# A hybrid encoder layer on one core: ScalarE's table load, the normalising of x, the memory norm and the start of the first scan head

## Chip, cores and metric

The kernel runs on one core of one Trainium2 chip. The metric is device time in microseconds (us) of one execution, and the median of the runs counts. Before the change it is 849.8 us (three runs, 849.77 to 851.0).

## What is computed

One encoder layer on x (512 tokens, width 1024, float32) and a memory of 256 tokens. For this change the first sub-layer matters:

```
h = rmsnorm(x, pre_mix_g)
aq, ak, av, hq, hf_fwd, hf_bwd, hi, hg = split_columns(h @ w_in)
att = axial_gqa_attention(apply_rope(aq), apply_rope(ak), av)
rec = hgrn2_group(hq, hf_fwd, hf_bwd, hi, hg, lb, out_g)     # 4 gated scan heads
x = x + rmsnorm(concat(att, rec) @ w_out, post_mix_g)
m = rmsnorm(mem, mem_norm_g)                                  # used by the second sub-layer
```

rmsnorm(x, g) is x · rsqrt(mean(x²) + eps) · g, with one factor r for each token. Cross-attention into m and a gated MLP with a small convolution follow; nothing in them changes.

## The kernel before, in words

**Arithmetic.** Each float32 operand of a product is split in two: a high part rounded to the matmul's type (ScalarE casts or scales, `hi`, `wh`) and the rest (VectorE subtracts, `lo`, `wl`). A product is then three matmuls, hi·hi, hi·lo, lo·hi (`mm3`, lines 135 to 137).

**Weights** come in 132 units of 128 x 1024. `issue()` (line 114) loads a unit into one of two `raw` buffers by a transfer of SyncE's queue, casts it on ScalarE (line 102) and subtracts on VectorE (line 103; units 28 to 41 on GpSimd). A `raw` buffer comes free with the subtraction of the unit two before. Units 0 to 3 feed the first projection (v), 4 to 6 the first scan head (q and its two gates, `hgrn_in(0)`), 7 to 10 the output gate (`put_sg`), then 11 to 13 scan head 1, and so on.

**Start.** x arrives transposed (`xt`, eight chunks kc of 128 x 512), together with the column `gcol` of pre_mix_g. WARM matmuls on constants (line 326) run until the first operands are there. `split_x(kc)` (lines 332 to 338) makes x·g in two parts: `nc.scalar.mul` by `gcol` on ScalarE, and one scalar_tensor_tensor (multiply, subtract) on VectorE. TensorE projects v from these raw parts (line 365), since r can be applied to a projection's result.

**r.** ScalarE squares the rows of x (line 378), GpSimd makes r (lines 153 and 154) and four diagonal tiles `diag_r` (line 382), TensorE spreads them over all partitions (line 385, ones times diagonal), and ScalarE copies the result to `r_bc` (line 387). v is scaled in `put_v` (line 430). The projections of head 0 also use raw x; `scaled` (line 435, VectorE) multiplies them by `r_bc`.

**The normalised x** (`hT`) for all later projections is made by `normalize(kc)` (lines 390 to 394), one for each chunk while head 0's projections are traced: VectorE makes t = xt·gcol·r_bc (line 392), ScalarE casts t (line 102), VectorE subtracts (line 103).

**Scan head h** (`hgrn_core`, lines 476 to 558): VectorE adds the two directions' keys (`ksum`, line 486), TensorE multiplies them with q (line 489), then seven levels follow. In each, VectorE updates queries and keys (line 525, twice), folds the gates (line 530) and takes the masked result over (line 531), ScalarE copies keys (line 496), and TensorE multiplies (line 499). Then come the two widest levels (lines 506 and 511 to 518), the output matmuls (537 to 539), a norm, the gate (line 549), and a turn (line 553).

**Memory norm** (`mem_norm`, lines 629 to 637): the gain and two blocks of 128 x 1024 come by transfers of GpSimd's queue (lines 148 and 634); ScalarE squares (line 188), GpSimd makes the factors (lines 153 and 154), VectorE scales (line 170).

**Order.** `weave` draws from two generators so that their announced progress stays level: the projections with the memory norm at their head (`mix_projections`), and the scan heads 0 to 2 (`cores`). From the traced program a scheduler sets the order of the instructions on each engine; at run time each engine takes its own in that order. `tc.issue_after(ins)` sets the instructions of a block behind `ins` on the engine of `ins`.

Of the kernel before, what the change touches and what calls it, by code (L numbers as in the profile page):

```python
# [14 lines left out]
ALU = mybir.AluOpType  # L15
# [3 lines left out]
P = 128  # L19
D = 1024  # L20
T = 512
# [10 lines left out]
TURN_STEP, MEM_TURN, UP_TURN = 0, (0, 4), (0, 2)  # L32
POOL_UNITS = frozenset(range(28, 42))
CORE_SHARE = 53.0
WARM = 4
LEVELS = (1, 2, 4, 8, 16, 32, 64)
ASK = 3
MIX_ORDER = (0, 2, 3, 1)
# [34 lines left out]
def layer(tc, io, out):  # L73
    nc = tc.nc
# [11 lines left out]
    def small():  # L86
        return sm.tile([P, 16], F32, name="small", tag="small")

    def bank(tag):
        return ps.tile([P, 512], F32, name="ps_" + tag, tag=tag)  # L90

    def big(shape, dt=F32):
        return b8.tile(shape, dt, name="big", tag="big")

    def tmp2(shape=(P, 512), dt=F32, tag="ta"):
        return t2.tile(list(shape), dt, name="tmp2", tag=tag, bufs=TMP_BUFS[tag])

    def tmp4(shape, dt=F32):
        return t4.tile(shape, dt, name="tmp4", tag="tmp4")

    def split(hi, lo, src, eng=None):
        nc.scalar.copy(hi, src)  # L102
        (eng or nc.vector).tensor_sub(lo, src, hi.bitcast(F32))  # L103
# [4 lines left out]
    def load_w():  # L108
        raw = rawp.tile([P, 1024], F32, name="raw", tag="raw")
        last_load[0] = nc.sync.dma_start(raw, io["w"][issued[0]]).ins  # L110
        issued[0] += 1
        return raw

    def issue():
        pool_unit = issued[0] in POOL_UNITS
        raw = load_w()
        wh = wp.tile([P, 1024], F32R, name="wh", tag="wh")
        wl = wp.tile([P, 1024], F32R, name="wl", tag="wl")
        split(wh, wl, raw, nc.gpsimd if pool_unit else None)
        pending.append((wh, wl))  # L120
# [7 lines left out]
    def unit(n):  # L128
        taken[0] += 1
        issue_ahead()  # L130
        wh, wl = pending.popleft()
        return wh.rearrange("p (k n) -> p k n", k=n), wl.rearrange("p (k n) -> p k n", k=n)

    def mm3(o, a, b, start, stop):
        nc.tensor.matmul(o, a[0], b[0], start=start, stop=False)  # L135
        nc.tensor.matmul(o, a[0], b[1], start=False, stop=False)  # L136
        nc.tensor.matmul(o, a[1], b[0], start=False, stop=stop)  # L137

    def blk(b):
        return slice(b * P, (b + 1) * P)  # L140
# [4 lines left out]
    def gains(*names, eng=None):  # L145
        g = big([P, 2, D])
        for i, name in enumerate(names):
            (eng or nc.gpsimd).dma_start(g[:, i, :], rows_bc(io[name], D))
        return [g[:, i, :] for i in range(len(names))]

    def rstd_of(ss, n, width):
        r = small()
        nc.gpsimd.tensor_scalar(r[:, :n], ss, 1.0 / width, EPS, op0=ALU.mult, op1=ALU.add)
        last_pow[0] = nc.gpsimd.tensor_tensor(out=r[:, :n], in0=r[:, :n], in1=nhalf[:, :n], op=ALU.pow).ins
        return r
# [13 lines left out]
    def scale_rows(xb, r, g, h, c):  # L169
        nc.vector.scalar_tensor_tensor(out=h[:, half(c)], in0=xb[:, half(c)], scalar=r, in1=g[:, half(c)],  # L170
                                       op0=ALU.mult, op1=ALU.mult)
# [14 lines left out]
    def row_rstd(xb, h):  # L186
        ss = small()
        nc.scalar.activation(h, xb, ACT.Square, accum_out=ss[:, 0:1])
        return rstd_of(ss[:, 0:1], 1, D)[:, 0:1]
# [32 lines left out]
    def new_act():  # L222
        return Act([big([P, 4, T], F32R) for _ in range(2)], [big([P, 4, T], F32R) for _ in range(2)])
# [23 lines left out]
    def proj_tm(act, tags, use, n=512):  # L247
        o = [bank(t) for t in tags]
        nk = 1024 // n
        for j in range(8 // nk):  # L250
            w = unit(nk)
            for b in range(len(tags)):
                for k in range(nk):
                    kc = nk * j + k
                    mm3(o[b][:, :n], act.get(kc, blk(b)), (w[0][:, k, :], w[1][:, k, :]), kc == 0, kc == 7)
                if kc == 7:
                    use(b, o[b])
                yield 3 * nk * MM * n / 512
# [41 lines left out]
    ident = const.tile([P, P], F32, name="ident")  # L300
    gcol = const.tile([P, KC], F32, name="gcol")
    ones = const.tile([P, P], F32, name="ones")
    nhalf = const.tile([P, 16], F32, name="nhalf")
    warm = tmp2()
    xt = [big([P, 4, T]) for _ in range(2)]
    nc.scalar.dma_start(gcol, io["gx"])
    nc.gpsimd.memset(ones, 1.0)
    nc.vector.memset(warm[:, :256], 0.0)
    nc.gpsimd.memset(nhalf, -0.5)

    def load_xt(kc, n):
        nc.sync.dma_start(xt[kc // 4][:, kc % 4:kc % 4 + n, :], io["xt"][:, kc:kc + n, :])
# [11 lines left out]
    warm_ps = bank("b")  # L324
    for _ in range(WARM):
        nc.tensor.matmul(warm_ps[:, :256], ones, warm[:, :256], start=True, stop=True)

    raw_act = new_act()

    after = []  # L330

    def split_x(kc):
        src = xt[kc // 4][:, kc % 4, :]
        hi, lo = raw_act.get(kc, slice(0, T))
        cast = nc.scalar.mul(hi, src, gcol[:, kc:kc + 1]).ins
        rest = nc.vector.scalar_tensor_tensor(out=lo, in0=src, scalar=gcol[:, kc:kc + 1], in1=hi.bitcast(F32),
                                              op0=ALU.mult, op1=ALU.subtract).ins
        return cast, rest
# [11 lines left out]
    v_ps = [bank(t) for t in "soso"]  # L350
    xr = room_x()
    ws = []
    for j in range(4):
# [7 lines left out]
        for k in range(2):  # L361
            kc = 2 * j + k
# [7 lines left out]
    ident_r = const.tile([P, P], F32R, name="ident_r")  # L370
    nc.vector.tensor_copy(ident_r, ident)
    taken[0] = 4
    for _ in range(2):
        issue()

    rx = const.tile([P, 2 * NB], F32, name="rx")
    for b in range(NB):
# [1 line left out]
    r = rstd_of(rx[:, :NB], NB, D)  # L379
    diag_r = tmp2((P, NB, P), tag="th")  # L380
    for b in range(NB):
        nc.gpsimd.tensor_scalar(diag_r[:, b, :], ident, r[:, b:b + 1], None, op0=ALU.mult)
    r_ps = bank("c")
    for b in range(NB):
        nc.tensor.matmul(r_ps[:, blk(b)], ones, diag_r[:, b, :], start=True, stop=True)
    r_bc = big([P, T])
    nc.scalar.copy(r_bc, r_ps)
    hT = new_act()

    def normalize(kc):  # L390
        t = tmp2()
        nc.vector.scalar_tensor_tensor(out=t, in0=xt[kc // 4][:, kc % 4, :], scalar=gcol[:, kc:kc + 1], in1=r_bc,
                                       op0=ALU.mult, op1=ALU.mult)
        split(*hT.get(kc, slice(0, T)), t)

    masks = const.tile([P, len(LEVELS), P], U8, name="masks")
    masks_f = tmp4([P, len(LEVELS), P])
# [23 lines left out]
    v = big([P, NB, T])  # L421
# [5 lines left out]
    sg_box, heads, qkv, rec_done = [], {}, {}, [0]  # L427

    def put_v(b, o):
        nc.scalar.mul(v[:, b, :], o, r[:, b:b + 1])  # L430

    def scaled(put):
        def use(o):
# [15 lines left out]
    def hgrn_in(h, between=(), raw=False):  # L449
        qk = big([P, 2, 2, T])  # L450
        tt = big([P, 2048])
        q = tmp2(tag="tq")

        def put_q(z):
            nc.scalar.activation(q, z, ACT.Sigmoid)
            nc.vector.tensor_mul(q, z, q)

        def put_f(d):
            def put(z):
                f = tt[:, d * T:(d + 1) * T]  # L460
                k = qk[:, 1, d, :]
                nc.scalar.activation(f, z, ACT.Sigmoid)
                nc.scalar.activation(k, z, ACT.Sigmoid, scale=-1.0)
                nc.vector.tensor_scalar(f, f, oml[:, d, h:h + 1], lb[:, d, h:h + 1], op0=ALU.mult, op1=ALU.add)
                nc.vector.tensor_scalar(k, k, oml[:, d, h:h + 1], None, op0=ALU.mult)
                nc.vector.tensor_mul(qk[:, 0, 1 - d, :], q, f)
            return put

        for put in (put_q, put_f(0), put_f(1)):
            yield from proj_fm(raw_act if raw else hT, T, "b", scaled(put) if raw else put)  # L470
            for job in between[:2]:
                job()
            between = between[2:]
        heads[h] = (q, qk, tt)
# [150 lines left out]
    tm_tags = ("s", "s", "o", "o")  # L625
# [3 lines left out]
    def mem_norm():  # L629
        g_mem, = gains("mem_norm_g")  # L630
        kv["rows"] = big([P, MB, D])
        for b in range(MB):
            m = kv["rows"][:, b, :]
            nc.gpsimd.dma_start(m, io["mem"][blk(b), :])
            r = row_rstd(m, tmp4([P, D]))
            for c in range(2):
                scale_rows(m, r, g_mem, m, c)
# [4 lines left out]
            turn_in(kv["rows"][:, b, :], kv["m"], b, "bb")  # L642

    def mix_projections():
        mem_norm()
        yield from proj_tm(hT, tm_tags, put_sg)
        yield from hgrn_in(1)
        yield from hgrn_in(2)
        mem_turn()
        yield from proj_tm(hT, tm_tags, put_kv, 256)  # L650
        late = []
        yield from proj_tm(hT, tm_tags, lambda b, z: late.append(lambda: put_qn(b, z)))
        yield from hgrn_in(3, late)

    def cores():
        for h in range(3):
            yield from hgrn_core(h)

    for b in range(NB):
        put_v(b, v_ps[b])  # L660
    for i, _ in enumerate(hgrn_in(0, raw=True)):
        if i < KC:
            normalize(i)
    weave((mix_projections(), 100.0), (cores(), CORE_SHARE))

    kT, vv, qT = qkv["kT"], qkv["vv"], qkv["qT"]
# [100 lines left out]
    hT = new_act()  # L767
# [75 lines left out]
    hT = new_act()  # L843
# [163 lines left out]
```

## Time and profile before

| | us |
|---|---|
| median of three runs | 849.8 |
| the profiled execution, its own time | 851.05 |
| its span, first to last instruction | 849.3 |
| TensorE busy | 828.8 (98% of the span) |
| VectorE busy | 526.6 (62%) |
| ScalarE busy | 401.1 (47%) |
| GpSimd busy | 95.9 (11%) |

The profile is of one execution; all its times count from the first instruction of its span. A row of the timeline has start, length, engine, line, operation, output and inputs, and in square brackets how long the engine was idle before it and what ended that. PE is TensorE, DVE VectorE, ACT ScalarE, POOL GpSimd, SP SyncE; a q behind the name (SPq) is the engine's queue. An engine's successive instructions overlap a little, so a start to the next start is somewhat less than a length.

### The profile page before, as it was taken

How to read it: one execution, taken by the hardware profiler on the slowest of the kernel's cores; microseconds unless marked ns; L12 is line 12 of the kernel's file. 1: busy time of each engine (PE TensorE's matmuls, PEld its weight loads, DVE VectorE, ACT ScalarE, POOL GpSimd, SP SyncE). 2: the span in 40 equal slices, each digit the busy share in tenths (PEclk: the TensorE clock that was granted, in tenths of full speed). 3: DMA queues.
4: the chain of work that ended last, by engine and by line, in shares of the span. 5: the costliest groups of instructions: out<-in, count | busy, mean ns of one | idle time of the engine just before them, and what ended most of it. 6: DMA issues, size and time to landing. Idle time of an engine off the chain costs nothing.

```text
span 849.3 us, 11048 instructions
## 1 busy us (share of the span) xinstructions
PE 828.8 (98%) x4304; PEld 702.9 (83%) x4304; DVE 526.6 (62%) x799; ACT 401.1 (47%) x710; POOL 95.9 (11%) x128
## 2 busy tenths in 40 slices
PE   8979999999999999999999999999999999999996
PEld 6868888887889888888888998888888888888885
DVE  5598497969997774854443865555555557722224
ACT  6563345445878884644543643333333335511121
POOL 0311100224243301300001300000000000000001
PEclk9999999999999999999999999999999999999999
DMA  9722202122222224252312242223233332322212
GB/s 323 232 76 75 74 25 87 51 76 75 75 75 91 78 81 175 75 174 75 100 50 75 76 135 98 95 94 100 100 100 99 100 100 79 101 96 97 100 49 100
DMA packets 24756, 83.52 MB, mean 98 GB/s; under 512 B 3264, under 2 KB 3904, under 8 KB 24704
## 3 DMA queue, kind: packets, MB, share of 16 engines
q1 hardware_dynamic: 22752, 77.44, 27.5%
q0 software_dynamic: 1232, 4.46, 1.7%
q10 hardware_dynamic: 720, 0.92, 0.3%
q8 instruction: 34, 0.56, 0.3%
q14 instruction: 18, 0.15, 0.1%
HBM read 80.71 MB, written 2.10 MB: 98 GB/s over the span
## 4 chain that ended last, share of the span: by engine, by line
PE 87%; DVE 6%; DMA 3%; ACT 2%; issue 1%; POOL 0%; POOLq 0%; DVEq 0%; ACTq 0%
PE ps_b L135 9%; PE ps_b L136 9%; PE ps_b L137 9%; PE ps_s L137 6%; PE ps_s L135 6%; PE ps_s L136 6%; PE ps_o L135 6%; PE ps_o L137 6%; PE ps_o L136 6%; PE ps_c L135 4%; PE ps_c L136 4%; PE ps_c L137 4%; PE ps_c L499 3%; DMA raw<-in_w_dram 2%; PE ps_o L717 2%; DVE big L525 1%
## 5 line engine op out<-in xcount | busy, mean ns | idle before, releaser
L103 DVE TENSOR_TENSOR wl<-raw,wh 128x1024 fp32r<-128x1024 f32 x114 | 139.4, 1223 | 219.7 <-ACT wh L102 219.6
L102 ACT CAST wh<-raw 128x1024 fp32r<-128x1024 f32 x128 | 134.6, 1052 | 243.5 <-PE ps_o L137 80.5
L135 PE MATMUL ps_b<-big,wh 128*128 128x512 f32 (+1 forms) x320 | 118.0, 369 | 0.0
L136 PE MATMUL ps_b<-big,wh 128*128 128x512 f32 (+1 forms) x320 | 116.6, 364 | 0.0
L137 PE MATMUL ps_b<-big,wl 128*128 128x512 f32 (+1 forms) x320 | 116.5, 364 | 0.0
L137 PEld LDWEIGHTS ps_b<-big,wl 128*128 128x128 f32 x320 | 60.3, 188 | 9.3
L135 PEld LDWEIGHTS ps_b<-big,wh 128*128 128x128 f32 x320 | 60.4, 189 | 9.1
L136 PEld LDWEIGHTS ps_b<-big,wh 128*128 128x128 f32 x320 | 60.4, 189 | 8.9
L163 POOL TENSOR_SCALAR small<-small 128x1 f32<-128x1 f32 x40 | 14.0, 350 | 440.6 <-ACT tmp L194 421.7
L135 PE MATMUL ps_s<-wh,big 128*128 128x512 f32 (+1 forms) x140 | 53.8, 384 | 0.0
L137 PE MATMUL ps_s<-wh,big 128*128 128x512 f32 (+1 forms) x140 | 53.4, 382 | 0.0
L136 PE MATMUL ps_s<-wl,big 128*128 128x512 f32 (+1 forms) x140 | 52.9, 378 | 0.0
L525 DVE TENSOR_TENSOR big<-big 128x512 f32<-128x512 f32 x64 | 49.8, 786 | 2.7 <-PE ps_c L499 1.6
L135 PE MATMUL ps_o<-wh,big 128*128 128x512 f32 (+1 forms) x124 | 47.5, 383 | 0.0
L137 PE MATMUL ps_o<-wh,big 128*128 128x512 f32 (+1 forms) x124 | 47.3, 381 | 0.0
L136 PE MATMUL ps_o<-wl,big 128*128 128x512 f32 (+1 forms) x124 | 47.1, 380 | 0.0
L103 DVE TENSOR_TENSOR big<-ps_o,big 128x512 fp32r<-128x512 f32 x52 | 35.8, 688 | 15.9 <-ACT big L102 15.5
L103 POOL TENSOR_TENSOR wl<-raw,wh 128x1024 fp32r<-128x1024 f32 x14 | 33.9, 2424 | 57.9 <-ACT wh L102 49.2
L102 ACT CAST big<-ps_o 128x512 fp32r<-128x512 f32 x52 | 30.4, 585 | 19.9 <-PE ps_o L814 7.5
L135 PE MATMUL ps_b<-wh,big 128*128 128x512 f32 x92 | 36.6, 398 | 0.0
L136 PE MATMUL ps_b<-wl,big 128*128 128x512 f32 x92 | 36.1, 392 | 0.0
L137 PE MATMUL ps_b<-wh,big 128*128 128x512 f32 x92 | 36.0, 391 | 0.0
(246 smaller groups left out, 1891.7 us busy)
## 6 DMA issues: line engine op xcount, KB each, us to landing
raw<-in_w_dram SPq DMA_DIRECT2D x131, 512.0 KB, 3.3
big<-in_x_dram SPq DMA_DIRECT2D x8, 512.0 KB, 7.3
big<-in_xt_dram SPq DMA_DIRECT2D x3, 512.0 KB, 8.0
big<-in_mem_dram POOLq DMA_DIRECT2D x2, 512.0 KB, 9.4
out_dram<-big SPq DMA_DIRECT2D x4, 256.0 KB, 2.1
out_dram<-big ACTq DMA_DIRECT2D x3, 256.0 KB, 2.1
big<-in_xt_dram SPq DMA_DIRECT2D x2, 256.0 KB, 3.4
raw<-in_w_dram SPq DMA_DIRECT2D x2, 256.0 KB, 4.0
```

The costliest lines, as they stand in the source:

```text
L102: nc.scalar.copy(hi, src)
L103: (eng or nc.vector).tensor_sub(lo, src, hi.bitcast(F32))
L135: nc.tensor.matmul(o, a[0], b[0], start=start, stop=False)
L136: nc.tensor.matmul(o, a[0], b[1], start=False, stop=False)
L137: nc.tensor.matmul(o, a[1], b[0], start=False, stop=stop)
L163: nc.gpsimd.tensor_scalar(ss[:, i + 4:i + 5], ss[:, i:i + 1], 1.0 / D, ss[:, i + 3:i + 4] if i else EPS, op0=ALU.mult, op1=ALU.add)
L499: nc.tensor.matmul(o[:, b, :], kc[:, blk(b)], pat(qk, b * P, [[2 * m, P // (2 * m)], [T + m, 2], [1, m]]), start=True, stop=True)
L525: nc.vector.tensor_tensor(out=c, in0=c, in1=pat(tt, toff + off, [[2, npair], [gap, 2], [0, m]]), op=ALU.mult)
L717: nc.tensor.matmul(o, vv[:, c, h // 4].rearrange("p a d -> p (a d)"), pt[:, j, c, :], start=c + j == 0, stop=c == 3 and j == 1)
```

## The change

Line numbers of the changed kernel are two higher than before from line 310 on, and nearly equal again from line 400 on. The diff, cut to its core:

```diff
-WARM = 4
+WARM, CORE_LEAD = 4, 3.0
...
     nc.gpsimd.memset(nhalf, -0.5)
+    table = small()
+    nc.scalar.copy(table, nhalf)
...
-    def split_x(kc):
+    def split_x(kc, act=raw_act):
         src = xt[kc // 4][:, kc % 4, :]
-        hi, lo = raw_act.get(kc, slice(0, T))
+        hi, lo = act.get(kc, slice(0, T))
...
     taken[0] = 4
-    for _ in range(2):
-        issue()
+    issue()
...
     for b in range(NB):
-        nc.gpsimd.tensor_scalar(diag_r[:, b, :], ident, r[:, b:b + 1], None, op0=ALU.mult)
+        nc.vector.tensor_scalar(diag_r[:, b, :], ident, r[:, b:b + 1], None, op0=ALU.mult)
...
-    nc.scalar.copy(r_bc, r_ps)
+    spread = nc.scalar.copy(r_bc, r_ps).ins
+    with tc.issue_after(spread):
+        issue()
     hT = new_act()
-
-    def normalize(kc):
-        t = tmp2()
-        nc.vector.scalar_tensor_tensor(out=t, in0=xt[kc // 4][:, kc % 4, :], scalar=gcol[:, kc:kc + 1], in1=r_bc,
-                                       op0=ALU.mult, op1=ALU.mult)
-        split(*hT.get(kc, slice(0, T)), t)
+    for i in range(4):
+        two = xt[i // 2][:, 2 * (i % 2):2 * (i % 2) + 2, :]
+        nc.gpsimd.tensor_tensor(out=two, in0=two, in1=r_bc[:, None, :].to_broadcast([P, 2, T]), op=ALU.mult)
...
     def mix_projections():
+        yield from proj_tm(hT, tm_tags, put_sg)
         mem_norm()
-        yield from proj_tm(hT, tm_tags, put_sg)
...
     def cores():
+        yield CORE_LEAD
         for h in range(3):
...
     for i, _ in enumerate(hgrn_in(0, raw=True)):
         if i < KC:
-            normalize(i)
+            split_x(i, hT)
```

So a copy of constants becomes ScalarE's first operation and brings the table load with it. Unit 5's cast stands behind the copy that makes `r_bc`. GpSimd multiplies xt by `r_bc` in place, in four instructions of 128 x 1024 (line 394), and `split_x` makes `hT` from that. The diagonal tiles are made by VectorE. The memory norm is traced behind the gate projection, and the scan heads announce 3.0 of progress before their first step.

On ScalarE, between the squares of x and the scaling of v (line 430), before the change:

```order
L378 ACTIVATE tmp_281,rx<-big 128x1024
L102 CAST wh<-raw 128x1024 x2
L415 ACTIVATE lbt<-lbt 128x16
L102 CAST wh<-raw 128x1024 x2
L387 COPY big<-ps_c 128x512
L430 ACTIVATE big<-ps_s,small 128x512
```

and with it, where L388 is the copy to `r_bc` and L337 the scaling in `split_x`:

```order
L379 ACTIVATE tmp_277,rx<-big 128x1024
L102 CAST wh<-raw 128x1024
L415 ACTIVATE lbt<-lbt 128x16
L388 COPY big<-ps_c 128x512
L102 CAST wh<-raw 128x1024
L430 ACTIVATE big<-ps_s,small 128x512
```

Three casts of weight units, 5 to 7, have moved from ahead of that copy to behind it.

On VectorE, the rows that lead to the first scan head (L486 is `ksum`), before:

```order
L103 TENSOR_TENSOR wl<-raw,wh 128x1024
L464 TENSOR_SCALAR big<-big,oml,lb 128x512
L465 TENSOR_SCALAR big<-big,oml 128x512
L466 TENSOR_TENSOR big<-tmp_332,big 128x512
L170 SCALAR_TENSOR_TENSOR big<-big,small 128x512 x4
L486 TENSOR_TENSOR tmp_520<-big 128x512
```

and where the memory norm's scaling (L170) stands now, far behind L486, which follows L466 at once; here L531 and L525 are steps of head 0's last levels, and L446 is the gate's product:

```order
L531 COPY_PREDICATED big<-masks,ps_c 128x4x128
L446 TENSOR_TENSOR big<-ps_o,tmp_674 128x512
L446 TENSOR_TENSOR big<-ps_o,tmp_695 128x512
L103 TENSOR_TENSOR wl<-raw,wh 128x1024
L170 SCALAR_TENSOR_TENSOR big<-big,small 128x512 x4
L525 TENSOR_TENSOR big<-big 128x2x2x128 x2
L103 TENSOR_TENSOR wl<-raw,wh 128x1024
```

The four L170 have moved from in front of the first head's first step to in front of its 128 wide level, for whose result TensorE's L511 waits. On VectorE from unit 5's subtraction to L486 there now stand six L103 of 128 x 1024, eight L338 (`split_x`), three L435, one L456, two each of L464, L465 and L466, and L486.

On GpSimd, from the masks (L409) on, with the change; before it the three transfers stood right behind L409 and no L394 existed:

```order
L409 CAST masks<-tmp_309 128x896
L394 TENSOR_TENSOR big<-big 128x1024 x4
L445 TENSOR_TENSOR tmp_643<-tmp_643,og 128x512
L148 DMA big<-in_mem_norm_g_dram 128x1024
L445 TENSOR_TENSOR tmp_653<-tmp_653,og 128x512
L634 DMA big<-in_mem_dram 128x1024
L445 TENSOR_TENSOR tmp_674<-tmp_674,og 128x512
L634 DMA big<-in_mem_dram 128x1024
L445 TENSOR_TENSOR tmp_695<-tmp_695,og 128x512
```

The memory's transfers have moved behind the products of the gate with its gain (L445), each of which waits for a sigmoid of the gate projection.

On TensorE, L489 (the first head's first product) stood behind 37 matmuls of the gate projection; it now stands behind 30 of its 96. L511 stood behind 84 of them; it now stands behind all 96 and 26 of the next projection.

More of the change, by code (lines that the diff above doesn't have):

```diff
@@ L429, in put_v @@
     def put_v(b, o):
-        nc.scalar.mul(v[:, b, :], o, r[:, b:b + 1])
+        return nc.scalar.mul(v[:, b, :], o, r[:, b:b + 1]).ins
     def scaled(put):
@@ L659, in layer @@
     for b in range(NB):
-        put_v(b, v_ps[b])
+        v_out = put_v(b, v_ps[b])
     for i, _ in enumerate(hgrn_in(0, raw=True)):
         if i < KC:
-            normalize(i)
+            split_x(i, hT)
     weave((mix_projections(), 100.0), (cores(), CORE_SHARE))
```

## The prediction

> **What bounds the kernel now.** TensorE is busy for 98% of the span, so what can be gained is where it waits or runs at a lower clock. I read TensorE's waits first, for the first 170 us, where every edit lies:
>
> ```profile
> PE ps_c L489 <- DVE tmp L486: 5.6, 1, 5.6
> ```
>
> One wait stands out: 5.6 us ahead of head 0's first product, for VectorE's `ksum`. The table by stretches shows what it costs besides (columns: length, then busy us of PE, PEld, DVE, ACT, POOL, then the granted clock):
>
> ```profile
> 50.00:56.00 6.00, 5.57 (x25) 4.29 (x23) 6.00 (x10) 3.67 (x7) 0.36 (x1) 1.00 0.28 90
> 56.00:62.00 6.00, 0.83 (x4) 0.83 (x5) 4.82 (x8) 2.26 (x4) 2.81 (x4) 0.90 0.28 87
> 62.00:70.00 8.00, 8.00 (x45) 7.09 (x45) 7.03 (x11) 3.19 (x5) 0.00 (x0) 0.86 0.19 66
> ```
>
> TensorE stands still in the second row, while the granted clock falls to 0.90 and then 0.86: 0.10 of 6 us and 0.14 of 8 us, another 1.7 us. VectorE was full before. Its timeline shows what stood in front of `ksum`:
>
> ```profile
> 57.24 1.41 DVE L170 SCALAR_TENSOR_TENSOR big<-big,small 128x512 f32<-128x512 f32 x2 [0.74 <-POOL small L154]
> 59.10 1.41 DVE L170 SCALAR_TENSOR_TENSOR big<-big,small 128x512 f32<-128x512 f32 x2 [0.44 <-POOL small L154]
> 60.43 0.68 DVE L486 TENSOR_TENSOR tmp<-big 128x512 f32<-128x512 f32 x1
> ```
>
> The memory norm, which nothing needs yet, holds VectorE for 4 us. The other place is the start, in the timeline of all engines:
>
> ```profile
> 0.72 0.40 ACTq L306 DMA_DIRECT2D gcol<-in_gx_dram  x1
> 1.26 3.75 PE L326 MATMUL ps_b<-tmp,ones 128*128 128x256 f32 x8 [1.26 <-DVE tmp L308]
> 3.81 1.28 ACT L335 ACT_TABLE_LOAD   x1 [3.81 <-DMA big<-in_xt_dram]
> 5.10 0.72 ACT L335 ACTIVATE big<-big,gcol 128x512 fp32r<-128x512 f32 x1
> 5.73 0.60 ACT L341 CAST wh<-raw 128x512 fp32r<-128x512 f32 x1
> 6.38 0.79 PE L365 MATMUL ps_s<-wh,big 128*128 128x512 f32 x1 [1.37 <-ACT wh L341]
> 9.11 0.63 PE L365 MATMUL ps_s<-wl,big 128*128 128x512 f32 x1
> 9.54 0.44 PE L365 MATMUL ps_o<-wl,big 128*128 128x512 f32 x1
> 9.81 0.40 PE L365 MATMUL ps_s<-wh,big 128*128 128x512 f32 x1
> ```
>
> The table load runs only once x has landed, 1.28 us on the path to the first matmul. And the first eight matmuls start 0.43 apart (9.11 to 9.54); the later ones take half of that.
>
> **The table load moved: -1.1 us.** It now runs before 3.8, while the transfers are under way. The first multiplication then waits for `gcol`, whose transfer took
>
> ```profile
> DMA to landing us min/median/max: 3.2/3.2/3.2
> ```
>
> from its issue at 0.72, so it starts at 3.92 instead of 5.10, and the first matmul at about 5.25 instead of 6.38. Bounds: 0 if the half unit of weights lands after 5.1, 1.28 at most. The second chunk's data are needed at a distance of 12 matmuls and have slack.
>
> **The clock at the start: -1.0 us.** TensorE's gap between warm-up and work shrinks from 1.37 to 0.25 us. In the rows the full pace came 3.4 us after the first real matmul; if that distance holds, nothing more is gained. If the warm-up now counts, up to eight steps fall from 0.43 to 0.23, 1.6 us. I take 1.0. The Trainium skill ("TensorE: Matmul & The Clock Gate", What's actually happening) states that the clock is released by one busy window of about 3.4 us, the windows running free of the kernel. By that rule the warm-up and the work would count together, and the sum would take the whole 1.6.
>
> **The diagonal tiles on VectorE, the copy ahead of unit 5's cast: 0.** These rows close the first projection:
>
> ```profile
> 29.54 0.39 PE L365 MATMUL ps_o<-wh,big 128*128 128x512 f32 x1
> 29.77 1.05 PE L385 MATMUL ps_c<-tmp,ones 128*128 128x128 f32 x8
> 30.58 0.48 PE L135 MATMUL ps_b<-big,wh 128*128 128x512 f32 x1
> 33.23 0.58 ACT L387 COPY big<-ps_c 128x512 f32<-128x512 f32 x1
> ```
>
> From 9.81 to 29.54 are 87 steps, 0.227 us each. L385 follows the last of them without idle time: its diagonal tiles are hidden behind the projection, on either engine. The copy, however, came 2.4 us after L385 had ended, behind casts that waited for weights; now it can follow at once. With the two gains at the start L385 begins near 27.7, and `r_bc` is there at 27.7 + 1.05 + 0.58 = 29.3. Unit 5's cast then ends near 30.3 rather than before 27; TensorE reaches that unit 24 matmuls (5.4 us) after 28.5, so the cast is covered by 3.6 us, less what follows.
>
> **x normalised by GpSimd: the wait for `ksum` comes back, +5.4 us, and half of the clock's loss, +0.9.** The work of VectorE on the way to `ksum`, by groups between 28 and 62 us (mean ns of one behind the comma):
>
> ```profile
> L103 DVE TENSOR_TENSOR wl<-raw,wh 128x1024 fp32r<-128x1024 f32 x5 | 6.1, 1221 | 5.2 <-ACT wh L102 5.2
> L392 DVE SCALAR_TENSOR_TENSOR tmp<-big,gcol 128x512 f32<-128x512 f32 x8 | 5.7, 743 | 0.0
> L435 DVE TENSOR_TENSOR tmp<-ps_b,big 128x512 f32<-128x512 f32 x3 | 2.0, 681 | 0.0
> L466 DVE TENSOR_TENSOR big<-tmp,big 128x512 f32<-128x512 f32 x2 | 1.4, 682 | 0.0
> L464 DVE TENSOR_SCALAR big<-big,oml,lb 128x512 f32<-128x512 f32 x2 | 1.1, 540 | 0.0
> L465 DVE TENSOR_SCALAR big<-big,oml 128x512 f32<-128x512 f32 x2 | 1.0, 478 | 0.0
> ```
>
> Eight L392 go (5.4 us at 0.08 less than a mean, the overlap of neighbours), and the L170 go. What stays, from unit 5's subtraction on: 6 x 1.14 (L103) + 8 x 0.67 (the new scalar_tensor_tensor, of L392's form) + 3 x 0.60 (L435) + 0.60 (L456) + 2 x (0.46 + 0.40 + 0.60) + 0.60 (L486) = 18.1 us. From 30.3 that would be done at 48.4. TensorE comes to L489 at 28.5 + (72 + 30) x 0.227 = 51.6, and would not wait.
>
> But the four multiplications on GpSimd meet this work. What happens then, other rows show:
>
> ```profile
> 238.24 2.70 POOL L103 TENSOR_TENSOR wl<-raw,wh 128x1024 fp32r<-128x1024 f32 x1 [3.44 <-DMA raw<-in_w_dram]
> 244.76 2.40 POOL L103 TENSOR_TENSOR wl<-raw,wh 128x1024 fp32r<-128x1024 f32 x1 [3.81 <-ACT wh L102]
> ...
> 238.00 0.68 DVE L525 TENSOR_TENSOR big<-big 128x512 f32<-128x512 f32 x1
> ...
> 239.62 0.69 DVE L103 TENSOR_TENSOR big<-ps_o,big 128x512 fp32r<-128x512 f32 x1
> 240.23 1.27 DVE L525 TENSOR_TENSOR big<-big 128x512 f32<-128x512 f32 x1
> ...
> 245.16 2.55 DVE L525 TENSOR_TENSOR big<-big 128x512 f32<-128x512 f32 x1
> ```
>
> An L525 with both inputs in SBUF takes 0.68 alone, but 2.55 when it starts 0.4 us into a GpSimd instruction of 2.40: it ends 0.55 after that one. The one at 240.23 ends likewise. The L103 at 239.62, which reads PSUM, is not held. And GpSimd, started during an L525, took 2.70. So the two run in turn, not together. L394 has the size of these 2.40 us instructions, and L445 takes half of that for half the size, with the same kind of broadcast operand:
>
> ```profile
> L445 POOL TENSOR_TENSOR tmp<-tmp,og x4: 1267/1276/1685, 81.8 to 87.3; 128x512 f32<-128x512 f32 x4
> ```
>
> Four of them are 9.6 us from 29.3 on. The first 1.0 passes before VectorE has unit 5's cast; the other 8.6 add to its 18.1: L486 ends at 57.0 instead of 48.4. The last `split_x`, ahead of L486, needs the last of them, so the order in which the two engines take turns does not change this. TensorE waits 57.0 - 51.6 = 5.4 us, at L489 or in part earlier (at unit 5's `wl`, or at unit 6 for the bank that the first L435 frees). Bounds: 3.6 if the three L435, which read PSUM, fall under GpSimd's turns, 0 if the engines overlap after all; I take 5.4, since of this work only the L435 read PSUM. The clock's 1.7 returns if the wait is in one piece, not if it is split; I take half. The Trainium skill ("SBUF - State Buffer", SBUF: two separate sides) calls this an exclusive lock, held for a whole instruction, and counts VectorE instructions with two SBUF inputs among those blocked; the 2.55 us above agrees.
>
> ScalarE multiplies (0.72) where it cast (about 0.63), 0.7 us in all, hidden behind its own idle time there.
>
> **The memory norm moved back: -5.6 and -1.7 for the old wait and its clock, +2.0 for a new one.** Its chain now begins with the gate's second sigmoid. Rows for it:
>
> ```profile
> 30.25 1.07 POOL L634 DMA_DIRECT2D big<-in_mem_dram  x2
> ```
>
> ```profile
> DMA to landing us min/median/max: 8.5/9.4/10.3
> ```
>
> ```profile
> raw<-in_w_dram SPq DMA_DIRECT2D x131, 512.0 KB, 3.3
> ```
>
> ```profile
> L188 ACT ACTIVATE tmp<-big x2: 1042/1044/1047, 54.4 to 55.4; 128x1024 f32<-128x1024 f32 x2
> ```
>
> ```profile
> L153 POOL TENSOR_SCALAR small<-small 128x1 f32<-128x1 f32 x2 | 1.7, 832 | 24.4 <-ACT tmp L188 24.3
> L154 POOL TENSOR_TENSOR small<-small,nhalf 128x1 f32<-128x1 f32 x2 | 1.5, 754 | 0.2
> ```
>
> Sigmoid 0.7 (as L335), L445 1.28, one issue 0.54, L445 1.28: the second block's transfer is issued 3.8 us after that sigmoid's matmuls. The same transfers took 9.4 us among the crowd at 30 us; a weight unit of their size takes 3.3. The queues are nearly empty there, so I take 4.0. Then the square 1.2, GpSimd 1.6, two L170 1.35, L525 0.7: 12.7 us in all. TensorE has 38 matmuls and three head products (0.81 each, as L385 to the next row) until L511: 11.0. So it waits 1.7, with GpSimd held up a little by VectorE 2.0; 1.0 to 7.1 by the transfer's bounds. While VectorE waits for these factors, L525, a unit's L103 and the next head's L456 queue behind L170; on ScalarE the copy of the head's wide result stands behind the square.
>
> **The sum.** -1.1 - 1.0 - 5.6 - 1.7 + 5.4 + 0.9 + 2.0 = -1.1 us, from 851.05 of the profiled execution. The median, 849.8, lies 1.25 below that one; I put the same -1.1 on it: **848.7 us**. A measurement here can tell about 0.2%, 1.7 us, from no change.
>
> **The rivals.**
> *The wait for `ksum` really goes* (0.26). GpSimd's work fits beside VectorE's, in its waits for casts and the L435. For it: VectorE had idle time there (5.2 us ahead of five L103). Against it: 240.23 and 245.16. Without 5.4 and 0.9: 842.4.
> *The memory's rows come late* (0.17), the slower side. If the transfers take the 9.4 us of before, L511 waits 7.1 instead of 2.0: 853.8. It turns slower by over 0.2% from a landing of 6.8 us on. For it: both were measured at 8.5 or more. Against it: the weights' 3.3.
> *The table load does not shorten the start* (0.07), since weights or the clock hold the first matmuls: 848.7 + 2.1 = 850.8.
>
> **How the numbers follow.** The forecast has 0.50, with a range of its own from 846.0 (L435 hidden, clock kept) to 851.0. Of it 0.19 lies below 848.1, 0.28 within 0.2% and 0.03 above 851.5. The first rival adds 0.26 to faster, the second 0.17 to slower, the third 0.04 to same and 0.03 to slower: faster 0.45, same 0.32, slower 0.23. The range, 842.0 to 853.0, takes in the first rival's time and most of the second's.
>
> **What would show it.** Right: the table load before 3.8; L365 from about 5.3; L394 of about 2.4 us, with L103 or L338 on VectorE beside them stretched to 2 us or more; TensorE waiting 4 to 6 us in all between 33 and 58 us for VectorE; one to three us ahead of L511. Wrong: L103 beside L394 at 1.22 and no wait at L489 (first rival); over 4 us ahead of L511 (second); the first L365 after 6.

## The result, and the profile after

The changed kernel takes 859.1 us (median of four runs, 857.0 to 859.5) against 849.8 before: a ratio of 1.0103, 95% interval 1.0083 to 1.0122, so about 9 us slower. Timed again on another chip it was 857.5 against 849.9: 1.0096 (1.0080 to 1.0112). The forecast was 848.7 and its range ended at 853.0.

The profiled execution after took 857.04 us with a span of 855.2. It is the fastest of its four, and the one shown of before (851.05, span 849.3) the slowest of its four, so the two traces lie only 6 us apart.

The start, from the timelines of ScalarE and TensorE (start, length, engine, line):

```profile
1.16 1.28 ACT L311 ACT_TABLE_LOAD   x1 [1.16 <-PEq L997]
...
3.83 0.72 ACT L337 ACTIVATE big<-big,gcol 128x512 fp32r<-128x512 f32 x1 [1.17 <-DMA gcol<-in_gx_dram]
...
5.11 0.79 PE L367 MATMUL ps_s<-wh,big 128*128 128x512 f32 x1
...
6.54 0.40 PE L367 MATMUL ps_o<-wh,big 128*128 128x512 f32 x1
6.77 0.40 PE L367 MATMUL ps_s<-wl,big 128*128 128x512 f32 x1
```

As forecast: the table load is out of the way, the first product comes at 5.11 instead of 6.38, and the full pace (0.23 from start to start) from 6.54 on instead of after 9.5. By 20 us the kernel is 2.1 us ahead of before.

TensorE's waits between 20 and 300 us (who waits, for whom; us in total, times, longest):

```profile
PE ps_b L135 <- DVE tmp L435: 4.8, 1, 4.8
PE ps_o L718 <- DVE big L103: 3.1, 3, 1.4
PE ps_c L499 <- DVE big L525: 2.7, 3, 1.3
PE ps_s L619 <- DVE tmp L103: 2.6, 2, 1.6
PE ps_c L511 <- DVE big L525: 1.8, 1, 1.8
PE ps_o L706 <- DVE big L103: 1.1, 2, 0.6
```

The 5.6 us at L489 are gone. In their place stands the wait that the forecast named, at unit 6 for the bank that L435 frees, and the one at L511. The other four rows are more than before had there (L717 1.9, L619 1.5, L499 0.7, none at L705). The first wait in the timeline of GpSimd and VectorE:

```profile
29.39 11.88 POOL L394 TENSOR_TENSOR big<-big 128x1024 f32<-128x1024 f32 x4 [1.29 <-ACT big L388]
...
30.29 2.60 DVE L103 TENSOR_TENSOR wl<-raw,wh 128x1024 fp32r<-128x1024 f32 x1 [2.14 <-ACT wh L102]
33.55 2.69 DVE L103 TENSOR_TENSOR wl<-raw,wh 128x1024 fp32r<-128x1024 f32 x1 [0.66 <-ACT wh L102]
36.16 6.33 DVE L338 SCALAR_TENSOR_TENSOR big<-big,gcol 128x512 fp32r<-128x512 f32 x3
...
43.54 0.68 DVE L435 TENSOR_TENSOR tmp<-ps_b,big 128x512 f32<-128x512 f32 x1
```

Four GpSimd instructions, of 2.4 us undisturbed, fill 11.88 us, and VectorE's subtractions, 1.22 alone, take 2.6 and more: one VectorE step to one of GpSimd, in turn.

So far all is near the plan, and yet 5 of the 6 us are still to come. The table by stretches, before (columns: length, busy us of PE, PEld, DVE, ACT, POOL, then the granted clock; the last line is the sum over 200 to 262 us):

```profile
210.00:220.00 10.00, 8.91 (x66) 8.44 (x66) 9.78 (x16) 7.88 (x15) 3.11 (x2) 1.00 0.18 54
230.00:240.00 10.00, 10.00 (x82) 9.61 (x81) 9.53 (x20) 8.83 (x19) 4.16 (x2) 1.00 0.28 100
...
sum 62.00, PE 57.29 PEld 52.49 DVE 57.56 ACT 46.76 POOL 23.60; mean PE 9.55 PEld 8.75 DVE 9.59 ACT 7.79 POOL 3.93
```

and after:

```profile
210.00:220.00 10.00, 8.37 (x53) 7.78 (x52) 9.86 (x10) 6.04 (x10) 5.20 (x2) 0.83 0.16 52
230.00:240.00 10.00, 7.30 (x58) 6.63 (x57) 10.00 (x18) 5.70 (x13) 3.59 (x2) 1.00 0.31 107
...
sum 62.00, PE 53.70 PEld 48.71 DVE 59.15 ACT 40.83 POOL 22.60; mean PE 8.95 PEld 8.12 DVE 9.86 ACT 6.80 POOL 3.77
```

TensorE does 57.29 - 53.70 = 3.6 us less in these 62 us, and ten of them run at a clock of 0.83, another 1.7. This is the start of attention beside scan head 3, over 100 us behind the work of the lines that the diff touches. VectorE is busy for 93% of it before and 95% after. The difference is in what it does while GpSimd makes the low part of a weight unit. After:

```profile
216.43 3.12 POOL L103 TENSOR_TENSOR wl<-raw,wh 128x1024 fp32r<-128x1024 f32 x1 [4.36 <-ACT wh L102]
228.30 2.39 POOL L103 TENSOR_TENSOR wl<-raw,wh 128x1024 fp32r<-128x1024 f32 x1 [8.75 <-ACT wh L102]
...
217.29 2.81 DVE L530 TENSOR_TENSOR big<-big 128x512 f32<-128x512 f32 x1
...
228.61 2.63 DVE L525 TENSOR_TENSOR big<-big 128x512 f32<-128x512 f32 x1 [0.54 <-PE ps_c L499]
```

and before:

```profile
226.36 2.41 POOL L103 TENSOR_TENSOR wl<-raw,wh 128x1024 fp32r<-128x1024 f32 x1 [4.72 <-ACT wh L102]
...
226.94 0.68 DVE L673 TENSOR_REDUCE small<-ps_s 128x1 f32<-128x512 f32 x1
227.53 0.68 DVE L103 TENSOR_TENSOR big<-ps_o,big 128x512 fp32r<-128x512 f32 x1
228.13 0.40 DVE L723 TENSOR_TENSOR tmp<-ps_o,tmp 64x256 f32<-64x256 f32 x1
```

Before, this subtraction falls beside VectorE steps that read PSUM (`ps_s`, `ps_o`), which run on at their 0.68. After, it falls on an L530 and an L525 whose inputs are both in SBUF, and each loses about 2 us. Summed over all of VectorE's rows between 200 and 262 us, the excess of the stretched ones (over 1.25 times the usual length of their form) is about 8 us before and 13.5 after. What GpSimd takes shows only as longer steps of VectorE: between 200 and 262 us of the changed kernel no wait that the profile lists for TensorE, VectorE or ScalarE ends with GpSimd or with a weight's transfer.

### The profile page after: what moved, and what is told of

It is laid out like the page before. It is cut to its first block, busy times and chain, and to the rows that moved or that the text cites. A ratio compares the mean times of both kernels' runs of the same rounds, so it can differ in the third digit from the quotient of the medians.

```text
span 855.2 us, 11032 instructions
## 1 busy us (share of the span) xinstructions
PE 829.8 (97%) x4304; PEld 704.0 (82%) x4304; DVE 536.2 (63%) x795; ACT 402.0 (47%) x711; POOL 106.0 (12%) x128
## 4 chain that ended last, share of the span: by engine, by line
PE 80%; DVE 7%; issue 6%; ACT 2%; DMA 2%; POOL 2%; SPq 0%; POOLq 0%; DVEq 0%
PE ps_b L137 8%; PE ps_b L135 8%; PE ps_b L136 8%; PE ps_s L136 6%; PE ps_s L137 6%; PE ps_s L135 6%; PE ps_o L135 5%; PE ps_o L137 5%; PE ps_o L136 5%; PE ps_c L136 4%; PE ps_c L135 4%; PE ps_c L137 4%; PE ps_c L499 2%; DVE big L525 2%; PE ps_o L718 2%
## 5 line engine op out<-in xcount | busy, mean ns | idle before, releaser
L103 DVE TENSOR_TENSOR wl<-raw,wh 128x1024 fp32r<-128x1024 f32 x114 | 142.2, 1247 | 212.1 <-ACT wh L102 212.0
L135 PE MATMUL ps_b<-big,wh 128*128 128x512 f32 (+1 forms) x320 | 118.8, 371 | 4.8 <-DVE tmp L435 4.8
L135 PEld LDWEIGHTS ps_b<-big,wh 128*128 128x128 f32 x320 | 60.9, 190 | 14.2 <-issue 5.2
L525 DVE TENSOR_TENSOR big<-big 128x512 f32<-128x512 f32 x64 | 53.8, 850 | 6.9 <-PE ps_c L499 4.7
L135 PE MATMUL ps_s<-wh,big 128*128 128x512 f32 (+1 forms) x140 | 54.1, 386 | 0.0
L135 PE MATMUL ps_o<-wh,big 128*128 128x512 f32 (+1 forms) x124 | 47.7, 385 | 0.0
L103 DVE TENSOR_TENSOR big<-ps_o,big 128x512 fp32r<-128x512 f32 x52 | 35.7, 686 | 16.0 <-ACT big L102 15.6
L103 POOL TENSOR_TENSOR wl<-raw,wh 128x1024 fp32r<-128x1024 f32 x14 | 34.8, 2486 | 62.1 <-ACT wh L102 51.8
L135 PE MATMUL ps_b<-wh,big 128*128 128x512 f32 x92 | 36.6, 398 | 0.0
```

The lines of the kernel that those rows point to most:

```text
L525: nc.vector.tensor_tensor(out=c, in0=c, in1=pat(tt, toff + off, [[2, npair], [gap, 2], [0, m]]), op=ALU.mult)
```

## Experiments

All ratios are to the kernel before, run on the same chip beside them, with the 95% interval; they go by all runs and can differ by 0.1% from the quotient of two medians. The theory after the comparison was A: the lead of the first core (`CORE_LEAD`) re-orders the whole stage from scan head 0 to scan head 3, and loses the time at 205 to 262 us. Its rivals were B, GpSimd's normalisation, and C, the memory norm.

**1. The table load alone**, on the kernel before.

```diff
+    table = small()
+    nc.scalar.copy(table, nhalf)
```

> Before, with the table load on a constant added and nothing else. Every theory expects the start's share alone: the load stands at about 1.2 us instead of behind the first tile, the first matmul of L365 comes about 1.2 us earlier, and the clock's early stretch costs less. 847.3 to 848.9 us (before: 849.8), unless an idle stretch later on eats it (then 849.8).

850.3 us, ratio 1.0003 (0.9990 to 1.0016): nothing. The trace (of an execution of 852.25 us, 2 us over the median) shows that the start does come earlier, by 1.8 us, and where the gain goes. Most of it goes before 31 us: TensorE comes to the diagonal tiles (L387 for L385) earlier than GpSimd has made them, and needs 2.2 us from its first L387 at 27.94 to L135, where it needed 0.8 before:

```profile
28.75 1.65 PE L387 MATMUL ps_c<-tmp,ones 128*128 128x128 f32 x6 [0.43 <-POOL tmp L384]
30.16 0.48 PE L135 MATMUL ps_b<-big,wh 128*128 128x512 f32 x1
```

The rest goes by 62 us, where the wait at `ksum` (here L491 for L488) is 6.3 us instead of 5.6. (The other piece, 0.4 us, stands ahead of scan head 3; before had 1.1 there.)

```profile
PE ps_c L491 <- DVE tmp L488: 6.7, 2, 6.3
```

ScalarE's timeline shows what that wait hangs on:

```profile
32.87 1.05 ACT L102 CAST wh<-raw 128x1024 fp32r<-128x1024 f32 x1 [5.72 <-DMA raw<-in_w_dram]
34.13 1.06 ACT L102 CAST wh<-raw 128x1024 fp32r<-128x1024 f32 x1 [0.21 <-DMA raw<-in_w_dram]
35.09 0.58 ACT L389 COPY big<-ps_c 128x512 f32<-128x512 f32 x1
```

`r_bc` (L389 here) stands behind two weight casts that wait for their transfers, and comes at 35.09 us, later than before (33.23) although TensorE has started earlier.

**2. The normalisation back on VectorE, the lead kept.**

```diff
-    for i in range(4):
-        two = xt[i // 2][:, 2 * (i % 2):2 * (i % 2) + 2, :]
-        nc.gpsimd.tensor_tensor(out=two, in0=two, in1=r_bc[:, None, :].to_broadcast([P, 2, T]), op=ALU.mult)
+    def normalize(kc):
+        t = tmp2()
+        nc.vector.scalar_tensor_tensor(out=t, in0=xt[kc // 4][:, kc % 4, :], scalar=gcol[:, kc:kc + 1], in1=r_bc,
+                                       op0=ALU.mult, op1=ALU.mult)
+        split(*hT.get(kc, slice(0, T)), t)
...
-            split_x(i, hT)
+            normalize(i)
```

> After, with the normalisation of x put back on VectorE as in before (no L394 on GpSimd, two VectorE steps and one ScalarE copy per chunk); table load, diagonal on VectorE, the moved memory norm and the lead of the first core stay. Theory A (the lead's new order of the mix stage loses the time at 205 to 262 us): the GpSimd stretch is gone and with it the wait of 4.8 us at L135 for L435, but the old wait at L489 comes back, so 855 to 859 us, little changed. Theory B (GpSimd's hold on VectorE sets everything later back): most of the loss goes, 848 to 852 us.

852.3 us, ratio 1.0024 (1.0011 to 1.0036): between the theories. GpSimd costs a good 6 us here, and the kernel is still slower than before. The old wait at L489, which A expected back, is only 0.7 us in this trace.

**3. Lead and memory norm back.**

```diff
-WARM, CORE_LEAD = 4, 3.0
+WARM, CORE_LEAD = 4, 0.0
...
-        yield from proj_tm(hT, tm_tags, put_sg)
         mem_norm()
+        yield from proj_tm(hT, tm_tags, put_sg)
```

> After, with the lead at 0 and the memory norm back at the head of the projections, so that only the table, the diagonal, the issue order and GpSimd's normalisation are changed. Theory A (the lead): about 850 to 853 us, the loss at 205 to 262 us is gone, since the order of the three tensor-side engines is that of before from the 260th row of TensorE on. Theory B (GpSimd's normalisation): 856 to 860 us, as after.

851.3 us, ratio 1.0013 (1.0002 to 1.0024): as A expected.

**4. The lead alone back** (the first pair of lines of that diff).

> After, with the lead of the first core at 0 and nothing else undone: the memory norm stays behind the gate's projection, the normalisation stays on GpSimd. Theory A (the lead): 850 to 854 us, within 1 us of the kernel that has the memory norm back as well. Theory B (GpSimd's normalisation) and theory C (the memory norm's late rows): 856 to 860 us; under C the kernel with the memory norm back is faster than this one by over 2 us.

849.9 us, ratio 0.9998 (0.9986 to 1.0010): A again, though 0.1 us under its range and 1.5 us from run 3 where it allowed 1; the lead costs 1.0096 - 0.9998 (the first from run 5), about 1% or 8.3 us. C falls: the moved memory norm is worth a little (0.15%, 1.3 us) rather than costing anything. The wait of 4.8 us at L135 stands in this kernel's trace as in the changed one's; the wait at L511 does not. By line and shape, the rows of TensorE, VectorE and ScalarE follow the order of before from 93 us on in this trace, and in the changed kernel's only from 239 to 249 us on.

That left a square with one corner open: without lead and without GpSimd's normalisation. A theory I, that each covers the other's wait, expected about 849; simple addition expected 843.

**5. The changed kernel again**, for the same chip.

> The changed kernel as it is, beside the others on the same chip: 857 to 860 us by every theory.

857.5 us, ratio 1.0096 (1.0080 to 1.0112).

**6. Lead and normalisation both back** (the edits of 2 and 4).

> After with the lead at 0 and the normalisation on VectorE both undone; table, diagonal on VectorE, issue order and the moved memory norm stay. It completes the square of lead and normalisation. Theory I (each wait covers the other: without the lead, GpSimd's normalisation puts the wait of 4.8 us at L135 in the place of the one of 5.6 us at L489, so that it costs next to nothing there, and costs 6.8 us only where the lead has taken the L489 wait away): 848 to 850 us, about the 849.9 of the kernel with the lead alone undone, and a wait of 5 to 6.5 us at L489. Theory S (the costs simply add, 9.2 us for the lead and 6.8 for GpSimd): 843 us.

843.3 us, ratio 0.9923 (0.9910 to 0.9935). Theory I falls: the costs add. The square, in per cent against before:

| | VectorE normalises | GpSimd normalises |
|---|---|---|
| no lead | -0.77 | -0.02 |
| lead of 3.0 | +0.24 | +0.96 |

The lead costs 1.0 in either column (8.3 to 8.6 us), GpSimd 0.7 to 0.75 in either row (6.1 to 6.4 us). And what is left of the change beats the kernel before by 6.6 us. The wait for head 0's `ksum` is gone altogether: the only one that its trace lists stands at 206.9 us, ahead of scan head 3, and before had the like there (1.1 us at 214.9):

```profile
PE ps_c L491 <- DVE tmp L488: 1.1, 1, 1.1
```

**7. and 8. GpSimd's weight subtractions replaced**, with the lead and without it. Both leave out the low part of units 28 to 41: it is set to zero.

```diff
-        split(wh, wl, raw, nc.gpsimd if pool_unit else None)
+        if pool_unit:
+            nc.scalar.copy(wh, raw)
+            nc.gpsimd.memset(wl.bitcast(F32), 0.0)
+        else:
+            split(wh, wl, raw)
```

> After, leaving out one piece of the computation: for the 14 weight units whose low part GpSimd subtracts (units 28 to 41), it writes zeros by a memset instead, in the same place of the same order, so that GpSimd reads nothing there. Theory D (the lead loses its time at 205 to 260 us because GpSimd's 2.4 us subtractions of L103 fall on more VectorE steps there, which this run's VectorE rows show stretched by 13.5 us in all, against 8.1 in before and 6.8 with the lead undone): it gains clearly more than the same cut in the kernel without the lead, so that the two lie 2 to 5 us apart instead of 9.2; about 848 to 852 us. Theory E (the lead's order itself runs dry there, whatever GpSimd does): gains as much as the other and stays 8 to 10 us above it.

> The same cut (zeros by a memset for GpSimd's 14 subtractions) in the kernel with the lead at 0. Both theories expect a gain from VectorE's stretches that go (6.8 us of stretches between 200 and 262 us, of which TensorE feels a part): 844 to 848 us. Theory D: this lies 2 to 5 us under the same cut with the lead; theory E: 8 to 10 us under it.

With the lead 846.4 us, ratio 0.9959 (0.9946 to 0.9971); without it 843.4, 0.9928 (0.9915 to 0.9942). Both gain more than either theory expected (848 and 844 us at the least). The two lie 3.0 us apart instead of 8.3: theory D. By line and shape, the order of 7 on TensorE, VectorE and ScalarE is the changed kernel's, row for row, so the order alone doesn't run dry there. The memsets still run on GpSimd, 0.96 us each:

```profile
L121 POOL MEMSET wl<- 128x1024 f32 x10 | 9.6, 956 | 48.1 <-PE ps_b L141 48.1
```

They read nothing, and VectorE's L525 beside them (mean ns behind the comma, between 200 and 262 us) is no longer stretched. After, then the same line, L529, in the lead's kernel with the memsets:

```profile
L525 DVE TENSOR_TENSOR big<-big 128x512 f32<-128x512 f32 x13 | 15.1, 1170 | 0.7 <-PE ps_c L499 0.5
```

```profile
L529 DVE TENSOR_TENSOR big<-big 128x512 f32<-128x512 f32 x16 | 11.6, 740 | 1.2 <-PE ps_c L503 0.6 <-PE ps_c L510 0.3 <-ACT tmp L500 0.2
```

The Trainium skill ("SBUF — State Buffer", Who interferes with whom) states just this: a VectorE instruction with two SBUF inputs contends with a GpSimd instruction that reads SBUF, not with one that only writes it. The 1,170 and 740 ns agree. The stage as a whole, TensorE's busy time between 200 and 262 us (first number behind the length), in the kernel of 4 (no lead, as 8 but with GpSimd's subtractions), then in 7, then in 8:

```profile
200.00:262.00 62.00, 56.94 (x427) 52.44 (x426) 57.34 (x102) 46.06 (x91) 21.26 (x9) 1.00 0.23 77
```

```profile
200.00:262.00 62.00, 61.71 (x460) 57.54 (x460) 56.99 (x115) 50.69 (x99) 11.71 (x12) 1.00 0.26 86
```

```profile
200.00:262.00 62.00, 62.00 (x465) 58.00 (x465) 55.12 (x113) 52.43 (x104) 9.23 (x10) 1.00 0.27 86
```

Without GpSimd's reads the stage is full with the lead (61.71) as without it (62.00); with them it holds 53.70 with the lead and 56.94 without. The 3 us that the lead still costs lie earlier: counted by matmuls, 7 is 2.8 us behind 8 at the 1,000th (192.9 and 190.1 us) and 3.4 at the 1,400th, while the changed kernel is 2.7 behind run 4's at the 1,000th and 8.0 at the 1,400th. L511 (1.7 us in 7's trace, none in 8's) is the largest part seen. The memset is also shorter than the subtraction that it replaces; as nothing waited for GpSimd in that stretch, this by itself doesn't explain the gain.

**9. and 10. What made the 6.6 us of gain?** From the kernel of 6, first the memory norm back (9):

```diff
-        yield from proj_tm(hT, tm_tags, put_sg)
         mem_norm()
+        yield from proj_tm(hT, tm_tags, put_sg)
```

and, apart from that, the issue order back (10):

```diff
-    issue()
+    for _ in range(2):
+        issue()
...
-    with tc.issue_after(spread):
-        issue()
```

> The kernel of 843.3 us (after with the lead at 0 and the normalisation on VectorE) with the memory norm back at the head of the projections, so that table, diagonal on VectorE and issue order are what is left of the change. Theory O (the issue order takes the wait of 5.6 us at L489: the spread copy of the row factors starts at 29.07 us instead of 35.09 behind two weight casts that wait for their DMA, and VectorE's normalisation with it): 843.5 to 846 us, the wait at L489 under 3.5 us. Theory M (the memory norm does, whose two scalings of 1.4 us stood ahead of L486 on VectorE): 848 to 850 us, the wait at L489 5 us or more.

> The kernel of 843.3 us with the issue order alone undone: both weight units are issued ahead of the squares again, and their casts stand ahead of the spread copy on ScalarE; table, diagonal on VectorE and the moved memory norm stay. Theory O (issue order): the spread copy starts at 33 to 35 us again, the wait at L489 is back with 3 to 5 us, 847 to 850 us. Theory M (memory norm): no wait over 2 us there, 843 to 845 us.

9 took 848.4 us, ratio 0.9980 (0.9971 to 0.9989); 10 took 846.7, 0.9969 (0.9956 to 0.9981). Both matter: 0.57% (4.8 us) for the memory norm and 0.46% (3.9 us; 3.1 by the medians) for the issue order. Together they are more than 6.6, so the parts don't simply add; the table and the diagonal were not taken out alone. By the time of 9 theory M had it, but not by its mechanism: no wait stands at `ksum`, but one of 3.1 us at L135. That the two scalings hold `ksum` up is not tested here, since in 9 the scheduler set them behind it (L488):

```profile
56.42 0.69 DVE L488 TENSOR_TENSOR tmp<-big 128x512 f32<-128x512 f32 x1
...
58.45 1.42 DVE L170 SCALAR_TENSOR_TENSOR big<-big,small 128x512 f32<-128x512 f32 x2 [0.73 <-POOL small L154]
```

ScalarE's and GpSimd's timelines in 9 show where the 3.1 us come from:

```profile
29.20 1.07 POOL L636 DMA_DIRECT2D big<-in_mem_dram  x2
...
39.18 1.04 ACT L102 CAST wh<-raw 128x1024 fp32r<-128x1024 f32 x1 [4.53 <-DMA raw<-in_w_dram]
```

VectorE's subtraction of this unit stands ahead of the step for which TensorE waits. The same cast in the kernel of 6:

```profile
35.43 1.05 ACT L102 CAST wh<-raw 128x1024 fp32r<-128x1024 f32 x1
```

With the memory norm at the head, its transfers are issued at 29 us, among the weights. Moved back, they leave the DMA queues to the weights: the DMA engines' share between 26 and 34 us falls from 0.82 to 0.37. In 10, `r_bc` is held by the casts again (32.86 instead of 29.07 us), and head 0's wait for `ksum` is back with 2.8 us. Its time is just under the 847 that theory O expected at the least.

**11. GpSimd's 14 weight subtractions on VectorE**, in the kernel of 6.

```diff
-POOL_UNITS = frozenset(range(28, 42))
+POOL_UNITS = frozenset()
```

> The kernel of 843.3 us with GpSimd's 14 subtractions (units 28 to 41) on VectorE: nothing on GpSimd stretches VectorE's steps any more (6.7 us of stretches between 200 and 262 us go), but seven subtractions of 1.22 us come to VectorE there (8.5 us). If a stretch costs what its length says, 844 to 846 us; if GpSimd's hold costs more than VectorE's rows show, under 842.5 us.

839.4 us, ratio 0.9876 (0.9863 to 0.9890), 10.5 us under before and the fastest of all. VectorE takes nine subtractions of 1.21 us more between 200 and 262 us, and TensorE is busy for 61.50 of the 62:

```profile
L103 DVE TENSOR_TENSOR wl<-raw,wh 128x1024 fp32r<-128x1024 f32 x9 | 10.9, 1213 | 0.1
```

By the bounds set beforehand GpSimd's hold would cost more than VectorE's rows show. But this isn't shown: the edit also alters the order of attention's instructions on TensorE and VectorE until about 280 us, and the run doesn't tell the two apart.

**12. GpSimd's normalisation in eight half steps**, without the lead.

```diff
-    for i in range(4):
-        two = xt[i // 2][:, 2 * (i % 2):2 * (i % 2) + 2, :]
+    for i in range(KC):
+        one = xt[i // 4][:, i % 4, :]
```

> After with the lead at 0 (849.9 us), with GpSimd's normalisation in eight steps of 512 columns instead of four of 1,024. If VectorE and GpSimd take turns step by step, as the rows show for the four, a VectorE step waits for half as long, and the subtractions of units 5 and 6 and the first chunk's come some 3 us earlier: the wait at L135 falls from 4.8 us to 1 to 3 us, 846 to 849 us. If GpSimd's steps run through in one piece once they are queued, or the fixed part of a step is large, the wait stays at 4 us or more: 849 to 851 us.

848.7 us, ratio 0.9985 (0.9976 to 0.9994), 1.1 us under the four steps of run 4 by the ratios; the wait at L135 fell from 4.8 to 3.7 only, not to the 1 to 3 that turns of half the length were to give:

```profile
30.00 14.31 POOL L394 TENSOR_TENSOR big<-big 128x512 f32<-128x512 f32 x8 [0.29 <-ACT big L388]
...
35.80 5.18 DVE L338 SCALAR_TENSOR_TENSOR big<-big,gcol 128x512 fp32r<-128x512 f32 x3
```

The turns are there, 1.73 us for a step of VectorE instead of 2.11, but there are more of them and GpSimd's whole stretch grows to 14.31. Smaller pieces shorten one hold, not their sum.

## Why the prediction was wrong

**The start (-1.1 and -1.0): right**, -2.1 us by 20 us: 1.3 for the first product and four of the eight slow steps. By itself it is worth nothing (run 1): in that trace the diagonal tiles, and then the casts that wait for transfers, take the gain back.

**The diagonal and the copy ahead of unit 5's cast (0): undersized.** The prediction saw that the copy came 2.4 us late "behind casts that waited for weights" and used the earlier `r_bc`, but gave it no worth of its own. Run 10 puts the issue order at 3.9 us. The diagonal tiles were hidden "on either engine" only as long as TensorE came late: in run 1, with the earlier start and GpSimd still making them, TensorE lost 1.4 us there. The diagonal was not tried alone.

**x normalised by GpSimd (+5.4 and +0.9): right** in mechanism and size. Measured in the square: 6.1 to 6.4 us, as 4.8 of waiting and a clock below 1 behind it:

```profile
40.00:46.00 6.00, 1.63 (x4) 1.38 (x5) 6.00 (x7) 3.83 (x5) 1.27 (x1) 0.84 0.21 69
46.00:52.00 6.00, 6.00 (x24) 4.86 (x24) 6.00 (x10) 2.93 (x5) 0.00 (x0) 0.88 0.33 109
```

(0.16 and 0.12 of 6 us: 1.7). The first rival, that GpSimd's work fits in beside VectorE's, is refuted by the stretched subtractions (2.60 and 2.69 us instead of 1.22) and this wait. The condition set for the clock's loss, a wait in one piece, held here, but is no rule: see the last section.

**The memory norm (-5.6, -1.7, +2.0): the old wait goes and the new one comes**, 1.8 us at L511 where 2.0 were forecast. But the reason given for the first was a part of it: by the rows of before, the L170 with their gaps fill 3.9 of the 5.6 us (56.50 to 60.43), and with no L170 there but the old issue order 2.8 us of wait remain (run 10). The memory's transfers among the weights cost on their own account (run 9), which the prediction didn't see. And the new wait goes with the lead: runs 4, 6 and 8, without it, have none at L511. The second rival, late memory rows, did not happen: they landed in 5.6 us.

**The step that failed is the sum's end.** The prediction read TensorE's waits "for the first 170 us, where every edit lies" and added them up to L511. It used the lead's order for the counts of matmuls ahead of L489 and L511, but put what `CORE_LEAD` does after that at nothing, with no other reason than this premise. It is the one edit that moves instructions through all of the stage to scan head 3. It costs 8.3 to 8.6 us (the square), and adding that to the forecast's -1.1 gives +7.3, near the +7.6 to +9.3 measured. That the rest of the sum comes out so well (-0.2 us in run 4, which lacks the lead alone) is in part luck: the memory norm, forecast at -5.3 in all, is worth 4.8 us beside VectorE's normalisation but 1.3 beside GpSimd's (runs 3 and 4), and the issue order, put at 0, is worth 3.9 where it was tried. Runs 7 and 8 show where most of the lead's cost comes from: 5.3 of the 8.3 us vanish when GpSimd reads nothing in units 28 to 41. The trace of before held the price already: the L525 of 2.55 us at 245.16, which the prediction quoted, but only for head 0. What stays open is why this order meets GpSimd's steps worse than the other; nothing in the kernel keeps the two apart in either.

One reading of the traces was wrong as well. Counted by matmuls, the changed kernel is level with before at the 1,000th (192.1 us in both) and 5.9 us behind at the 1,400th (258.3 and 252.4), so that GpSimd's normalisation seemed to cost nothing. Set against run 2, whose order on TensorE is all but the same, it falls behind by 6.5 us at 40 us and is 6.0 behind at 200. Level with before meant that the gains of the start, the issue order and the memory norm had just paid for it.

## What to carry to other kernels

An edit that shifts one stream of an interleaved schedule is priced where the streams meet at the bound engine, not where the edit stands: look there for what a changed order will put side by side. Work given to GpSimd that reads SBUF can cost VectorE nearly GpSimd's own length where VectorE's steps read both inputs from SBUF (2 us of 2.4 at the L525 above); 2.4 us there were dearer than 1.2 us on VectorE in run 11, which changed the order too. Undo the edits of a mixed change one by one: here the rest of the change gained 6.6 us, and two parts gave back 15.

## What the hardware showed beyond that

Back-to-back GpSimd instructions don't keep VectorE out, nor VectorE them: where both have a step ready they alternate one for one (11.88 us for 4 x 2.40, 14.31 for eight halves). A wait need not be long to cost clock: between 210 and 220 us of the changed kernel the waits are pieces of at most 1.6 us, and the granted clock still fell to 0.83. Nor does the length of a wait alone decide it. Run 12 and run 4 both have a wait of 1.55 us at L619 that ends at 204 us; the clock that follows (the third number from the end) is 0.79 in the first and 1.00 in the second:

```profile
204.00:212.00 8.00, 7.97 (x50) 7.36 (x51) 5.55 (x9) 4.98 (x7) 2.39 (x1) 0.79 0.17 50
```

```profile
204.00:212.00 8.00, 6.88 (x51) 6.27 (x51) 6.65 (x10) 4.99 (x8) 2.42 (x1) 1.00 0.21 68
```

So 1.7 us of clock may come or not with a wait of this kind, and a difference of that size between two single traces needs the medians beside it. What decides it is not shown.

A VectorE step with one large SBUF input can be held too: L464, a multiplication by columns, takes 0.54 us alone, and 2.11 and 2.22 in the changed kernel (at 203.1 and 210.1 us) beside GpSimd's subtractions.
